# Multiplying every third tap of a depthwise convolution on GpSimd

## The chip, the core and the metric

The kernel runs on one core of one Trainium2 chip. Its engines are TensorE (PE in the profile; PEld is its weight load), VectorE (DVE), ScalarE (ACT), GpSimd (POOL) and SyncE (SP, which issues most transfers). The metric is the device time of one execution in microseconds. A measurement of the kernel is the median of several executions.

## What is computed

The reference is a trunk of two layers over a sequence of 256 positions with 2048 channels, in float32. Each layer normalises the input, modulates it by a vector c, projects it with one matrix into 13 pieces of 512 channels, sends these through four mixers (Fourier, neighbourhood attention, retention, convolution), gates and concatenates the results, and projects them back.

```
for l in range(DEPTH):                                   # 2 layers
    mod = c_act @ w_ada[l] + b_ada[l]                    # (3 x 2048)
    h = _rmsnorm(x, norm_g[l]) * (1.0 + scale) + shift
    z = h @ w_in[l]                                      # 256 x 2048 @ 2048 x 6656
    ...
    o_cv = _conformer_conv(cv_a, cv_b, ...) * silu(cv_g)
    y = concatenate([o_fft, o_na, o_ret, o_cv]) @ w_out[l]
    x = x + gate * y

def _conformer_conv(a, b, conv_w, conv_b, ln_g, ln_b, w_pw):
    u = a * sigmoid(b)
    y = depthwise_conv(u, conv_w, width 31, centred) + conv_b   # 512 channels, each its own 31 weights
    y = layernorm(y) * ln_g + ln_b
    return silu(y) @ w_pw
```

The change lies in the depthwise convolution: y[s, ch] is the sum over 31 taps t of conv_w[t, ch] * u[s + t - 15, ch].

## The kernel before

**Weights.** Nearly all time is matrix products of the normalised input with streamed weights. A weight step loads 256 rows by 512 columns (512 KB) into one of eight buffers named raw. ScalarE casts it to a high part `whi` (line 340), VectorE subtracts that from the loaded values to get a low part `wlo` (line 341), and TensorE makes three products of high and low parts with the high and low parts of the input, `hh` and `hl` (lines 358 to 361 where the result has channels on partitions, 390 to 392 where it has positions there). Four split weight steps can be ahead of TensorE.

**Modulation.** The product of c with w_ada is made on VectorE: each step loads 128 rows of 1024 numbers into the same raw buffers, and one VectorE instruction multiplies them with c, spread over the partitions (`cbc`), and sums (line 515; the row `DVE_READ_ACCUMULATOR2_ANT` belongs to it). These steps are merged between the weight steps.

**The mixers.** Each mixer is a Python generator that is advanced by a pacer once per weight step, so that its instructions lie between those of the weight steps. The convolution starts when its two input pieces are there (`uT`, 128 channels on partitions times 4 blocks of channels, 256 positions with 15 zeros on both sides). Its sum `y` (tile `cy`) has 4 blocks of 256 positions. In the code before, a tap is made in one of two ways:

- Where t is not a multiple of 3, ScalarE multiplies the shifted input by the tap's weight, a number per partition, into a product tile `cvp` of two blocks (128x2x256, line 684; two such buffers take turns), and VectorE adds the product to the sum, two blocks at once (line 688, 128x512).
- Where t is a multiple of 3 and not 0, which is ten taps in a layer, VectorE multiplies and adds in one instruction per block (line 672, 128x256, four of them).

A tap yields to the pacer twice, after half its work and at its end; the pace is 2 yields per weight step in layer 0 and 1.5 in layer 1.

**What sets the order.** The program is written in the order of the generators, and a scheduler then puts each engine's instructions into a fixed order from its own estimate of when they are ready. Each engine works through its list in that order. A change of one instruction's engine can thus move others.

**GpSimd** does little before: some small powers (lines 212, 219, 707, 977), and four pairs of transfers that spread the gates (lines 538 and 540).

Of the kernel before, what the change touches and what calls it, by code (L numbers as in the profile page):

```python
# [11 lines left out]
F32 = mybir.dt.float32  # L12
F32R = mybir.dt.float32r
AF = mybir.ActivationFunctionType
ALU = mybir.AluOpType
AX = mybir.AxisListType

P = 128
S = 256
# [72 lines left out]
def trunk(ctx, tc, x, c, cols, w_ada, w_in, w_fft, na_bias, consts, conv_w_pw, w_out, final_g, out):  # L92
    nc = tc.nc
    V, A, G, T = nc.vector, nc.scalar, nc.gpsimd, nc.tensor

    sb = ctx.enter_context(tc.tile_pool(name="sb", bufs=1))
# [3 lines left out]
    def bank(tag, name):  # L100
        return ps.tile([P, 512], F32, tag=tag, name=name)

    def wide(tag, name):
        return sb.tile([P, 1024], F32, tag=tag, name=name)

    def ta(name, n=512):
        return sb.tile([P, 512], F32, tag="ta", name=name, bufs=3)[:, :n]
# [4 lines left out]
    def small(name, n, bufs=4):  # L112
        return sb.tile([P, n], F32, name=name, bufs=bufs)
# [461 lines left out]
    def h_cva(l, z):  # L575
        def f():
            for b in range(2):
                V.scalar_tensor_tensor(z[b], flags["t"][b], 1.0, z[b], op0=ALU.add, op1=ALU.mult)
            pacer.add("conv", conv(l), PACE["conv"][l])
        later(1, f)  # L580
# [84 lines left out]
    def conv(l):  # L665
        uT = T4[CVA]
        y = wide("cvA", "cy").rearrange("p (k s) -> p k s", k=4)
        w = cwt[:, l].rearrange("p (w k) -> p w k", k=4)
        for t in range(CW):
            if t and t % 3 == 0:  # L670
                for b in range(4):
                    V.scalar_tensor_tensor(y[:, b], uT[:, b, t:t + S], w[:, t, b:b + 1], y[:, b],  # L672
                                           op0=ALU.mult, op1=ALU.add)
                    if b == 1:
                        yield
            else:
                for b in range(0, 4, 2):
                    d = sb.tile([P, 2, S], F32, tag="cvp", name="cvp", bufs=2) if t else y[:, b:b + 2]
                    for i in range(2):
                        if t == 0:  # L680
                            A.activation(d[:, i], uT[:, b + i, 0:S], AF.Identity, scale=w[:, 0, b + i:b + i + 1],
                                         bias=prm[:, 4 * l + b + i:4 * l + b + i + 1])
                        else:
                            A.activation(d[:, i], uT[:, b + i, t:t + S], AF.Copy, scale=w[:, t, b + i:b + i + 1])  # L684
                    if b == 0:
                        yield
                    if t:
                        V.tensor_tensor(y[:, b:b + 2], y[:, b:b + 2], d, op=ALU.add)  # L688
            yield
        yn = wide("cvU", "yn").rearrange("p (m n) -> p m n", m=2)  # L690
        bs, mvs, rss = [], [], []
        yield
        for m in range(2):
            b = bank("mx", "cvt")
            for k in range(4):
                T.transpose(b[:, k * P:(k + 1) * P], y[:, k, m * P:(m + 1) * P], ident)
            bs.append(b)
        yield
        yield
        for m in range(2):  # L700
            st = small("cst", 6)
            mv = small("cmv", 2)
            rs = small("crs", 1)
            V.bn_stats(st, bs[m])
            V.bn_aggr(mv, st)
            V.tensor_scalar(rs, mv[:, 1:2], EPS, None, op0=ALU.add)
            G.tensor_tensor(rs, rs, nhalf[:, :1], op=ALU.pow)
            mvs.append(mv)
            rss.append(rs)
        yield  # L710
        yield
        for m in range(2):
            if m < YNA:
                off = small("cof", 1)
                V.scalar_tensor_tensor(off, mvs[m][:, 0:1], -1.0, rss[m], op0=ALU.mult, op1=ALU.mult)
                A.activation(yn[:, m], bs[m], AF.Identity, scale=rss[m], bias=off)
            else:
                V.tensor_scalar(yn[:, m], bs[m], mvs[m][:, 0:1], rss[m], op0=ALU.subtract, op1=ALU.mult)
        yield
        yield  # L720
        y2 = wide("cvA", "cy2").rearrange("p (k s) -> p k s", k=4)
        for k2 in range(2):
            b = bank("mx", "cvt2").rearrange("p (k s) -> p k s", k=2)
            for k in range(2):
                for m in range(2):
                    T.transpose(b[:, k, m * P:(m + 1) * P], yn[:, m, (2 * k2 + k) * P:(2 * k2 + k + 1) * P], ident)
            t = ta("cth2").rearrange("p (k s) -> p k s", k=2)
            for k in range(2):
                i = 4 * l + 2 * k2 + k
                A.activation(t[:, k], b[:, k], AF.Tanh, scale=lnh[:, i:i + 1], bias=lnh[:, 8 + i:9 + i])  # L730
                A.activation(y2[:, 2 * k2 + k], b[:, k], AF.Identity, scale=prm[:, 8 + i:9 + i],
                             bias=prm[:, 16 + i:17 + i])
            yield
            yield
            V.scalar_tensor_tensor(y2[:, 2 * k2:2 * k2 + 2], t, 1.0, y2[:, 2 * k2:2 * k2 + 2],
                                   op0=ALU.add, op1=ALU.mult)
        while flags.get(CVG) != l or "fft" in pacer.gens:
            yield "wait"
        yield from pointwise(conv_w_pw[l], y2, T4[CVG].rearrange("p (k s) -> p k s", k=4), 0.25)
# [9 lines left out]
    def pointwise(w, y, g, factor):  # L749

        wt = load_small(w)
        for _ in range(4):
            yield
        b = None
        for o in range(4):
            k2, k = divmod(o, 2)
            if k == 0:
                old, b = b, bank("mx", "pwb").rearrange("p (k s) -> p k s", k=2)
            for kt in range(4):
                T.matmul(b[:, k], wt[kt // 2][:, kt % 2, o * P:(o + 1) * P], y[:, kt], start=(kt == 0),  # L760
                         stop=(kt == 3))
            yield
            if k == 1:
                V.scalar_tensor_tensor(g[:, 2 * k2:2 * k2 + 2], b, factor, g[:, 2 * k2:2 * k2 + 2],
                                       op0=ALU.mult, op1=ALU.mult)
# [535 lines left out]
```

## Time and profile before

| | us |
|---|---|
| median of 3 runs | 952.18 |
| lowest and highest run | 949.46, 954.27 |
| profiled execution | 955.11 |
| its span, first to last instruction | 953.3 |
| TensorE busy | 902.8 (95%) |
| VectorE busy | 780.6 (82%) |
| ScalarE busy | 591.0 (62%) |
| GpSimd busy | 22.2 (2%) |
| transfers, mean rate | 272 GB/s |

The profile is one execution. Its page lists busy time of each engine, the span in 40 slices (a digit is the busy share in tenths), the costliest groups of instructions, and the chain of work that ended last. A group's row has the line, the engine, the operation, what it writes and reads, shape and count, then the busy time of the group and the mean of one instruction in ns, then the idle time of the engine just before these instructions and what ended it. Busy time of a group counts overlapping records once. A row of the timeline has start, duration, engine, line and operation; in brackets stands the idle time before it and what released it. A row of waits names who waited for whom, then the total in us, the number of waits and the longest. A table of stretches has, behind the length of the stretch, busy time and number of instructions of each engine.

### The profile page before, as it was taken

The numbers are of one execution on the slowest core, as the hardware profiler recorded it, in microseconds if no ns is written. First come the engines' busy times: TensorE is split into PE (matmuls) and PEld (weight loads), VectorE is DVE, ScalarE is ACT, GpSimd is POOL, SyncE is SP. The second block draws the span as 40 slices with busy tenths as digits, with TensorE's granted clock in tenths as the row PEclk, the third lists the DMA queues.
The fourth block names the chain that finished last, engine by engine and source line by source line (L and its number), as shares of the span: only waits on it lengthen the run. The fifth ranks groups of instructions, "written<-read, shape, count | busy, mean of one in ns | idle before, by whom it ended". The sixth has DMA issues, their size and how long they took to land.

```text
span 953.3 us, 14695 instructions
## 1 busy us (share of the span) xinstructions
PE 902.8 (95%) x5294; PEld 769.1 (81%) x5294; DVE 780.6 (82%) x1266; ACT 591.0 (62%) x1019; POOL 22.2 (2%) x31
## 2 busy tenths in 40 slices
PE   4789999999998999999999999999999999999995
PEld 1779799898976786778878999999778889788874
DVE  5988989889998999888878798558987977578963
ACT  4488855779776766544644464669899645643441
POOL 2000000000000010010000000000000000010000
PEclk6899999999999999999999999999999999999998
DMA  9999997897786777979876999777755576479932
GB/s 338 397 399 376 362 399 276 297 381 246 262 272 237 245 268 264 309 255 337 305 251 194 320 373 381 243 245 231 234 179 163 183 251 188 128 247 328 325 118 88
DMA packets 109068, 259.68 MB, mean 272 GB/s; under 512 B 8386, under 2 KB 10562, under 8 KB 108740
## 3 DMA queue, kind: packets, MB, share of 16 engines
q1 hardware_dynamic: 108292, 256.64, 77.8%
q0 software_dynamic: 704, 2.11, 0.6%
q8 instruction: 41, 0.67, 0.3%
q14 instruction: 31, 0.25, 0.1%
HBM read 256.61 MB, written 2.11 MB: 271 GB/s over the span
## 4 chain that ended last, share of the span: by engine, by line
PE 54%; DMA 18%; DVE 17%; issue 6%; ACT 4%; POOL 1%; DVEq 0%; SPq 0%; POOLq 0%; ACTq 0%
PE acc L361 9%; PE acc L358 9%; PE acc L360 9%; DMA raw<-in_w_in_dram 9%; PE acc L390 7%; PE acc L391 7%; PE acc L392 7%; DVE wlo L341 7%; DMA raw<-in_w_ada_dram 6%; DVE raw L515 4%; DMA raw<-in_w_out_dram 2%; ACT whi L340 1%; PE pwb L760 1%; DMA xs<-in_x_dram 1%; PE nao L828 1%
## 5 line engine op out<-in xcount | busy, mean ns | idle before, releaser
L340 ACT ACTIVATE whi<-raw 128x1024 fp32r<-128x1024 f32 (+1 forms) x272 | 277.6, 1028 | 185.6 <-PE acc L392 89.1
L341 DVE TENSOR_TENSOR wlo<-raw,whi 128x1024 fp32r<-128x1024 f32 (+1 forms) x272 | 319.9, 1182 | 49.4 <-ACT whi L340 47.9
L515 DVE CUSTOM_DVE_ANT_0 raw<-raw,cbc 128x1024 f32<-128x1024 f32 x192 | 232.8, 1221 | 48.4 <-DMA raw<-in_w_ada_dram 48.3
L358 PE MATMUL acc<-hh,whi 128*128 128x256 f32 x896 | 255.8, 286 | 10.1 <-ACT hh L286 7.3
L360 PE MATMUL acc<-hl,whi 128*128 128x256 f32 x896 | 252.7, 283 | 2.4 <-DVE hl L299 2.4
L361 PE MATMUL acc<-hh,wlo 128*128 128x256 f32 x896 | 252.2, 284 | 1.7 <-DVE wlo L341 1.1
L391 PE MATMUL acc<-wlo,hh 128*128 128x512 f32 x600 | 239.5, 399 | 3.0 <-DVE wlo L341 2.8
L390 PE MATMUL acc<-whi,hh 128*128 128x512 f32 x600 | 242.2, 406 | 0.0
L392 PE MATMUL acc<-whi,hl 128*128 128x512 f32 x600 | 238.7, 398 | 0.0
L358 PEld LDWEIGHTS acc<-hh,whi 128*128 128x128 f32 x896 | 169.2, 189 | 15.7 <-ACT hh L286 7.7
L360 PEld LDWEIGHTS acc<-hl,whi 128*128 128x128 f32 x896 | 170.1, 190 | 3.3 <-DVE hl L299 2.7
L361 PEld LDWEIGHTS acc<-hh,wlo 128*128 128x128 f32 x896 | 169.1, 190 | 2.9 <-DVE wlo L341 2.8
L391 PEld LDWEIGHTS acc<-wlo,hh 128*128 128x128 f32 x600 | 114.0, 190 | 31.0 <-DVE wlo L341 5.4
L390 PEld LDWEIGHTS acc<-whi,hh 128*128 128x128 f32 x600 | 113.4, 190 | 29.6 <-issue 4.6
L392 PEld LDWEIGHTS acc<-whi,hl 128*128 128x128 f32 x600 | 113.7, 189 | 27.0
L459 ACT ACTIVATE z<-acc 128x512 f32<-128x512 f32 x99 | 57.4, 598 | 36.1 <-PE acc L361 20.1
L684 ACT ACTIVATE cvp<-uT,constants 128x256 f32<-128x256 f32 x160 | 70.6, 500 | 12.2 <-DVE cy L688 12.1
L688 DVE TENSOR_TENSOR cy<-cy,cvp 128x512 f32<-128x512 f32 x80 | 52.5, 688 | 1.6 <-ACT cvp L684 1.5
L430 ACT ACTIVATE acc<-z 128x512 f32<-128x512 f32 x63 | 36.5, 599 | 0.3
L672 DVE SCALAR_TENSOR_TENSOR cy<-uT,constants,cy 128x256 f32<-128x256 f32 x80 | 34.7, 480 | 0.1
L205 ACT ACTIVATE junk<-xs 128x512 f32<-128x512 f32 x16 | 9.5, 593 | 35.9 <-DVE xs L484 35.9
L483 DVE TENSOR_TENSOR yt<-acc,gate_bc 128x512 f32<-128x512 f32 x16 | 10.4, 684 | 12.5 <-PE acc L392 12.5
(211 smaller groups left out, 703.4 us busy)
## 6 DMA issues: line engine op xcount, KB each, us to landing
raw<-in_w_in_dram SPq DMA_DIRECT2D x198, 512.0 KB, 5.2
raw<-in_w_ada_dram SPq DMA_DIRECT2D x192, 512.0 KB, 6.1
raw<-in_w_out_dram SPq DMA_DIRECT2D x64, 512.0 KB, 6.0
raw<-in_w_in_dram SPq DMA_DIRECT2D x20, 256.0 KB, 6.7
nab<-in_na_bias_dram SPq DMA_DIRECT2D x16, 192.0 KB, 3.6
xs<-in_x_dram SPq DMA_DIRECT2D x2, 1024.0 KB, 5.9
gate_bc<-gate_row POOLq DMA_DIRECT2D x4, 512.0 KB, 5.1
wsm<-in_w_fft_dram SPq DMA_DIRECT2D x4, 512.0 KB, 5.4
```

The source lines that it names most:

```text
L340: self.on_act = A.activation(self.hi[:, :n], self.raw[:, :n], AF.Copy).ins
L341: self.on_dve = V.tensor_tensor(self.lo[:, :n], self.raw[:, :n], self.hi[:, :n].bitcast(F32), op=ALU.subtract).ins
L358: T.matmul(o, wh[:, sl], hh[:, k], start=fresh and blk % 2 == 0 and blk // 2 not in g.seeded, stop=False, skip_group_check=True)
L360: T.matmul(o, wh[:, sl], hl[:, k], start=False, stop=False, skip_group_check=True)
L361: T.matmul(o, wl[:, sl], hh[:, k], start=False, stop=en, skip_group_check=True)
L390: T.matmul(o, hh[:, k, sl], wh, start=st, stop=False, skip_group_check=m in g.seeded)
L391: T.matmul(o, hh[:, k, sl], wl, start=False, stop=False, skip_group_check=m in g.seeded)
L392: T.matmul(o, hl[:, k, sl], wh, start=False, stop=en, skip_group_check=m in g.seeded)
L459: A.activation(o, i, AF.Copy, scale=0.125 if last and self.piece == NAQ else 1.0)
L515: V.tensor_tensor_reduce(w, w, cbc[:, self.half * KH:(self.half + 1) * KH], 0.5, 0.0, ALU.mult, ALU.add, to)
L684: A.activation(d[:, i], uT[:, b + i, t:t + S], AF.Copy, scale=w[:, t, b + i:b + i + 1])
L688: V.tensor_tensor(y[:, b:b + 2], y[:, b:b + 2], d, op=ALU.add)
```

## The change

In the taps that are multiples of 3, the four fused multiply-adds of VectorE are replaced. GpSimd multiplies each of the four blocks by the tap's weight into a product tile, and VectorE adds two blocks at once. The product tiles are called `cvq` and come from the same two buffers as ScalarE's products (tag `cvp`).

```
         for t in range(CW):
             if t and t % 3 == 0:
-                for b in range(4):
-                    V.scalar_tensor_tensor(y[:, b], uT[:, b, t:t + S], w[:, t, b:b + 1], y[:, b],
-                                           op0=ALU.mult, op1=ALU.add)
-                    if b == 1:
+                for b in range(0, 4, 2):
+                    d = sb.tile([P, 2, S], F32, tag="cvp", name="cvq", bufs=2)
+                    for i in range(2):
+                        G.tensor_scalar(d[:, i], uT[:, b + i, t:t + S], w[:, t, b + i:b + i + 1], None, op0=ALU.mult)
+                    if b == 0:
                         yield
+                    V.tensor_tensor(y[:, b:b + 2], y[:, b:b + 2], d, op=ALU.add)
             else:
                 for b in range(0, 4, 2):
                     d = sb.tile([P, 2, S], F32, tag="cvp", name="cvp", bufs=2) if t else y[:, b:b + 2]
```

The lines after it are two further down in the changed kernel: the addition of ScalarE's product is line 688 before and 690 after; GpSimd's product is line 674 and its addition line 677.

The order on VectorE at the start of layer 0's convolution, taps 2 to 6, before:

```order
L688 TENSOR_TENSOR cy<-cy,cvp 128x512 x2
L341 TENSOR_TENSOR wlo<-raw,whi 128x1024
L672 SCALAR_TENSOR_TENSOR cy<-uT,constants,cy 128x256 x4
L341 TENSOR_TENSOR wlo<-raw,whi 128x1024
L688 TENSOR_TENSOR cy<-cy,cvp 128x512 x2
L341 TENSOR_TENSOR wlo<-raw,whi 128x1024
L688 TENSOR_TENSOR cy<-cy,cvp 128x512 x2
L672 SCALAR_TENSOR_TENSOR cy<-uT,constants,cy 128x256
L341 TENSOR_TENSOR wlo<-raw,whi 128x1024
L672 SCALAR_TENSOR_TENSOR cy<-uT,constants,cy 128x256 x3
```

and the same taps after:

```order
L690 TENSOR_TENSOR cy<-cy,cvp 128x512 x2
L341 TENSOR_TENSOR wlo<-raw,whi 128x1024
L677 TENSOR_TENSOR cy<-cy,cvq 128x512 x2
L341 TENSOR_TENSOR wlo<-raw,whi 128x1024
L690 TENSOR_TENSOR cy<-cy,cvp 128x512 x2
L515 ISA raw,msum<-raw,cbc 128x1024
L515 ISA msum 128x1
L341 TENSOR_TENSOR wlo<-raw,whi 128x1024
L690 TENSOR_TENSOR cy<-cy,cvp 128x512 x2
L341 TENSOR_TENSOR wlo<-raw,whi 128x1024
L677 TENSOR_TENSOR cy<-cy,cvq 128x512 x2
```

The additions of GpSimd's products stand where the fused instructions stood, one split (line 341) behind the additions of the tap before; GpSimd can write a product's buffer only after those. One modulation product (line 515) has moved up among them.

The order on GpSimd from the first convolution to the end of layer 0, after:

```order
L674 TENSOR_SCALAR cvq<-uT,constants 128x256 x17
L538 DMA gate_row<-gcol 128x8
L674 TENSOR_SCALAR cvq<-uT,constants 128x256 x3
L540 DMA gate_bc<-gate_row 128x1024
L674 TENSOR_SCALAR cvq<-uT,constants 128x256 x20
L538 DMA gate_row<-gcol 128x8
L540 DMA gate_bc<-gate_row 128x1024
L709 TENSOR_TENSOR crs<-crs,nhalf 128x1 x2
```

Before, the four transfers stood there with nothing between them. Now the first pair stands among the products of the fifth multiplied tap and behind it, and the second pair behind all 40 products of the layer. In layer 1 all 40 products stand ahead of the transfers.

## The prediction

> **What bounds the kernel now.** I read the first two parts of the page, then the two stretches in which the convolution runs, then who waits there, then GpSimd's own rows.
>
> ```profile
> span 953.3 us, 14695 instructions
> PE 902.8 (95%) x5294; PEld 769.1 (81%) x5294; DVE 780.6 (82%) x1266; ACT 591.0 (62%) x1019; POOL 22.2 (2%) x31
> PE   4789999999998999999999999999999999999995
> DVE  5988989889998999888878798558987977578963
> ```
>
> TensorE is busy from the third slice to the last but one. Its ends are modelled, so I also look at how close its matmuls start in the chain of waits, in the first convolution:
>
> ```profile
> 217.06 0.23 PE acc L390
> 217.29 0.23 PE acc L391
> 217.53 0.23 PE acc L392
> ```
>
> They follow each other at 0.23 us with no gap. TensorE is the bound here; another engine costs time only by letting it run dry. The convolution's instructions lie in 205 to 340 us (layer 0) and 640 to 760 us (layer 1). A table of busy time in these two stretches (engines in the order of its first row):
>
> ```profile
> core 0: us, PE busy (x) PEld busy (x) DVE busy (x) ACT busy (x) POOL busy (x), PEclk, DMA share, GB/s
> 205.00:340.00 135.00, 130.51 (x770) 109.68 (x769) 128.37 (x247) 108.29 (x220) 1.85 (x3) 0.99 0.79 263
> 640.00:760.00 120.00, 116.97 (x738) 100.59 (x737) 103.08 (x198) 106.05 (x221) 0.00 (x0) 1.00 0.64 201
> ```
>
> TensorE idles 4.5 us in the first and 3.0 us in the second: 7.5 us is all that a lighter VectorE could win back there. VectorE idles 6.6 us in the first and 16.9 us in the second. In the first it is as full as TensorE, and it decides when the weight buffers come free, since the split into high and low parts (line 341) and the modulation products (line 515) are the last readers of each loaded tile. The chain of waits shows that loop, from a convolution instruction over a split to the next load and the next cast:
>
> ```profile
> 258.65 1.58 DVE cy L672 x4
> 260.24 1.15 DVE wlo L341
> 261.40 6.11 DMA raw<-in_w_in_dram
> 267.59 1.06 ACT whi L340
> ```
>
> So in layer 0 a later VectorE is a later load. In layer 1 its idle time is mostly waiting for inputs:
>
> ```profile
> DVE raw L515 <- DMA raw<-in_w_ada_dram: 6.9, 5, 1.9
> DVE sm L809 <- ACT nasb L804: 3.2, 3, 1.5
> DVE z L833 <- PE nao L828: 2.6, 3, 1.5
> ```
>
> **The change, part by part.** Ten of the 31 taps in each layer (3, 6, ... 30) lose four fused multiply-adds on VectorE and get four multiplications on GpSimd and two additions on VectorE.
>
> ```profile
> L688 DVE TENSOR_TENSOR cy<-cy,cvp 128x512 f32<-128x512 f32 x80 | 52.5, 688 | 1.6 <-ACT cvp L684 1.5
> L672 DVE SCALAR_TENSOR_TENSOR cy<-uT,constants,cy 128x256 f32<-128x256 f32 x80 | 34.7, 480 | 0.1
> ```
>
> Removed: 80 instructions, 34.7 us busy, 0.434 us each where they overlap their neighbours. Added: 40 additions of 128x512, the form of the first row, at 52.5/80 = 0.656 us, so 26.2 us. VectorE's own work falls by 8.5 us, 4.2 us in each layer.
>
> GpSimd gets 80 multiplications of 128x256, a form that this trace does not have. The nearest rows are those where it works over a whole tile, and its one-element multiply, first with VectorE idle and then beside it:
>
> ```profile
> L176 POOL IOTA diff<- 128x384 f32 x1 | 0.4, 448 | 0.0
> masks.py:199 POOL TENSOR_SCALAR_AFFINE_SELECT ident<-ident 128x128 f32<-128x128 f32 x1 | 0.3, 285 | 0.0
> 11.75 0.19 POOL L211 TENSOR_SCALAR ms<-ms 128x1 f32<-128x1 f32 x1
> 15.01 1.06 POOL L211 TENSOR_SCALAR ms<-ms 128x1 f32<-128x1 f32 x1
> 14.80 1.22 DVE L515 CUSTOM_DVE_ANT_0 raw<-raw,cbc 128x1024 f32<-128x1024 f32 x1
> 15.94 1.22 DVE L515 CUSTOM_DVE_ANT_0 raw<-raw,cbc 128x1024 f32<-128x1024 f32 x1
> 17.09 1.22 DVE L515 CUSTOM_DVE_ANT_0 raw<-raw,cbc 128x1024 f32<-128x1024 f32 x1
> ```
>
> Low end: 0.19 us fixed and the affine select's slope, (0.285 - 0.19)/128 per element, is 0.38 us for 256 elements. High end: twice the affine select, 0.57 us. I take 0.45 us, near the middle, since no row favours either end: 40 x 0.45 = 18.0 us of GpSimd in each layer.
>
> The last five rows price what it does to VectorE. The same one-element instruction took 0.19 us with VectorE idle and 1.06 us while VectorE worked on two operands in SBUF: issued at 15.01, it ended at 16.07, just after the VectorE instruction that began at 14.80 gave way to the next at 15.94. GpSimd waited for its turn and got it between two VectorE instructions. VectorE started at 14.80, 15.94 and 17.09, 1.14 and 1.15 us apart, so a one-element GpSimd instruction cost it nothing that shows; what a 256-element one costs it no row shows. The ends are nothing and the whole 0.45 us. I take the whole: what keeps GpSimd out while VectorE works should keep VectorE out while GpSimd works, and where it does not, the addition that needs the product is the next or next but one on VectorE's queue (the rows in the part on the change) and waits for it there. Nearly everything VectorE does in these stretches, line 341, line 515 and the additions, has two operands in SBUF.
>
> The Trainium skill (SBUF — State Buffer, section "Who interferes with whom") goes further than the row: a VectorE instruction with two SBUF inputs and a GpSimd instruction that reads SBUF hold the shared ports in turn, each for its whole instruction. By it VectorE pays the whole 18.0 us in each layer; by the spacing of the VectorE rows alone it would pay nothing. The trace agrees on GpSimd's side (1.06 us against 0.19 us) and does not show VectorE's.
>
> VectorE's sum in each layer is then 18.0 - 4.2 = 13.8 us more (0.38 us: 11.0; 0.57 us: 18.6; no block: 4.2 less). What of it reaches TensorE is what the idle time does not hold. Layer 0: of 6.6 us I count half as usable, 3.3, because much of it is waiting for casts whose loads hang on VectorE itself: 10.5 us reach the end. Layer 1: of 16.9 us I count two thirds, 11.3, because the modulation products and the attention inputs that it waits for come whatever it does: 2.5 us. Together 13.0 us. After 340 us TensorE is full again to the next layer, so nothing is won back.
>
> What costs nothing. The additions use the two product buffers that ScalarE's products use, so ScalarE's next product waits for the addition of GpSimd's product; ScalarE idles 26.7 us of the first stretch and makes a half tap in two products, so this hides as long as the additions are not themselves late. GpSimd's two gate transfers now stand among its products:
>
> ```profile
> 256.68 0.74 POOL L538 DMA_DIRECT2D gate_row<-gcol  x1 [239.10 <-DVE gcol L537]
> 260.43 0.56 POOL L540 DMA_DIRECT2D gate_bc<-gate_row  x1 [3.01 <-ACT cvp L684]
> ```
>
> One product stands behind the first (0.74 us, once). The second, with its 3.0 us of waiting, follows the twentieth product, the end of a tap; the next is needed three taps later, about 12 us (135/31 a tap). In layer 1 the transfers come after the products.
>
> The sum against the profiled execution: 955.1 us (span 953.3 and 1.8 around it) + 13.0 = 968.1 us. That execution was 2.9 us above the median of the runs, 952.18 us; taken off, 965 us.
>
> **The rivals.** All in the median's frame, 952.2.
>
> *The turns are short.* If GpSimd keeps VectorE out only while it moves data, 0.45 - 0.19 = 0.26 us, the sum is 10.4 - 4.2 = 6.2 us in each layer: 2.9 us left in layer 0 and none in layer 1, 955 us. For it: VectorE's start times did not move above. Against it: the additions wait for whole products, not for the shared part. The Trainium skill (GPSIMD Engine Reference, section 4.1 "Engine selection") calls GpSimd's one-input work roughly line-rate; its 1.2 GHz makes that, as an estimate, 0.21 us for 256 elements, and the sum by it is 1.0 us in layer 0 and nothing in layer 1. No row here shows a one-input GpSimd instruction over 256 elements.
>
> *Relief.* If the two do not meet at all, VectorE has 8.5 us less to do. This is the faster side, and it is limited by TensorE's idle time in the two stretches, 7.5 us, whose largest pieces are these, the first two in layer 0:
>
> ```profile
> PE nas L784 <- ACT napt L820: 2.5, 1, 2.5
> PE pwb L760 <- DVE nm L796: 1.1, 1, 1.1
> PE ff L856 <- ACT ffb L872: 1.4, 1, 1.4
> PE ff L856 <- ACT z L459: 1.4, 2, 0.7
> ```
>
> ScalarE's lateness goes back to VectorE through loads like that at 261.40, so I let 6 us fall away: 946 us. For it: VectorE is on the chain in layer 0. Against it: the 1.06 us row, and that most of these waits name ScalarE.
>
> *No slack is usable.* If VectorE's waits move along with it, because the loads it waits for start only when it frees their buffers, as at 260.24 above, both sums arrive whole: 2 x 13.8 = 27.6 us, 980 us. It decides once TensorE has used the split weights made ahead (four tiles). For it: VectorE waits for a modulation tile 6.9 us in layer 1. Against it: in the middle of layer 1's stretch VectorE idles over 3 us in 20 us (third number 16.53 and 16.81), and TensorE is full all the same:
>
> ```profile
> 700.00:720.00 20.00, 19.75 (x103) 14.68 (x102) 16.53 (x47) 19.05 (x47) 0.00 (x0) 1.00 0.52 161
> 720.00:740.00 20.00, 20.00 (x139) 16.46 (x138) 16.81 (x32) 18.94 (x40) 0.00 (x0) 1.00 0.53 159
> ```
>
> **How the numbers follow.** Forecast 0.50 (965 us); short turns 0.25 (955 us); no slack 0.14 (980 us); relief 0.11 (946 us). About 0.5%, 4.8 us, is what a measurement of this kernel can tell from no change: 947.4 to 956.9 us. Slower is the forecast and no slack, 0.64. Same is short turns and the weakest part of relief, 0.02: 0.27. Faster is the rest, 0.09. The range runs from 949, which keeps out most of relief, to 985, the forecast's two sums at the long GpSimd duration with little slack (955.1 + 37.2 - 3.3 - 2.9 = 986). The forecast's own range is 960 to 975, the ends of GpSimd's duration through the same sum: 0.38 us leaves 7.7 us in layer 0 and nothing in layer 1, 0.57 us 15.3 and 7.3 us.
>
> **What would show it.** GpSimd: 80 multiplications, each recorded at 0.4 to 1.3 us, since the wait for the turn is in the record (as in the 1.06 us row). VectorE: 40 additions on GpSimd's products at 0.65 us, and VectorE waiting for GpSimd before them, some 5 to 15 us in all; its splits at line 341 longer than the 1.22 us of now, or starting more than 1.14 us apart, only in the two stretches. The stretch from the first product to the last addition is 10 us longer in layer 0 and 2 to 5 us in layer 1, with TensorE's waits for the low parts of the weights, in layer 0 these two, up from 0.9 us:
>
> ```profile
> PE acc L361 <- DVE wlo L341: 0.7, 1, 0.7
> PE acc L391 <- DVE wlo L341: 0.2, 1, 0.2
> ```
>
> Wrong would be: splits that keep 1.14 us beside GpSimd's products (then relief or short turns), a multiplication far from 0.38 to 0.57 us when VectorE stands still, or a loss that lies outside the two stretches.

## The result

The changed kernel took 982.91 us, median of 3 runs (979.02 to 983.2), against 952.18 us before: a ratio of 1.032 with a 95% interval of 1.029 to 1.036. It is slower by 30.7 us. The prediction was 965 us; the direction was right, the loss more than twice as large. Its profiled execution took 983.2 us. One execution of an experiment below ran at a granted clock of 0.84 instead of 0.98 and is left out of that experiment's median.

The head of its page and three groups of instructions:

```profile
span 981.4 us, 14829 instructions
PE 915.3 (93%) x5294; PEld 777.7 (79%) x5294; DVE 779.6 (79%) x1226; ACT 591.9 (60%) x1019; POOL 129.9 (13%) x111
POOL 2000000024443310010000000004532420010000
L674 POOL TENSOR_SCALAR cvq<-uT,constants 128x256 f32<-128x256 f32 x80 | 106.9, 1350 | 488.7 <-DVE cy L690 471.6 <-DVE gcol L537 8.5 <-ACT whi L340 7.7
L686 ACT ACTIVATE cvp<-uT,constants 128x256 f32<-128x256 f32 x160 | 71.0, 499 | 38.9 <-DVE cy L677 28.8
L677 DVE TENSOR_TENSOR cy<-cy,cvq 128x512 f32<-128x512 f32 x40 | 29.3, 735 | 34.6 <-POOL cvq L674 34.5
```

The last row carries the result. VectorE's 40 additions of GpSimd's products took 29.3 us, but VectorE stood still for 34.5 us in front of them, waiting for GpSimd. GpSimd's 80 multiplications were recorded at 1.35 us each. ScalarE in turn waited 28.8 us for those additions, because the two share product buffers.

The first such tap on VectorE and GpSimd, from the timeline (start, duration, idle time before):

```profile
214.40 1.22 DVE L341 TENSOR_TENSOR wlo<-raw,whi 128x1024 fp32r<-128x1024 f32 x1
217.27 0.96 DVE L677 TENSOR_TENSOR cy<-cy,cvq 128x512 f32<-128x512 f32 x1 [1.66 <-POOL cvq L674]
219.07 0.69 DVE L677 TENSOR_TENSOR cy<-cy,cvq 128x512 f32<-128x512 f32 x1 [0.84 <-POOL cvq L674]
219.68 1.22 DVE L341 TENSOR_TENSOR wlo<-raw,whi 128x1024 fp32r<-128x1024 f32 x1
```

```profile
213.98 2.35 POOL L674 TENSOR_SCALAR cvq<-uT,constants 128x256 f32<-128x256 f32 x1 [195.61 <-DVE cy L690]
216.32 0.92 POOL L674 TENSOR_SCALAR cvq<-uT,constants 128x256 f32<-128x256 f32 x1
217.22 0.92 POOL L674 TENSOR_SCALAR cvq<-uT,constants 128x256 f32<-128x256 f32 x1
218.12 0.92 POOL L674 TENSOR_SCALAR cvq<-uT,constants 128x256 f32<-128x256 f32 x1
```

GpSimd is released at 213.98, when the first of the two shared buffers is free. Its first product takes 2.35 us, because VectorE is working: an addition to 214.40 and then a split to 215.6. The other three take 0.92 us each. VectorE, whose next instruction needs the first two products, is idle from 215.6 to 217.27, and again between the two additions. From the split's start at 214.40 to the next split at 219.68 pass 5.28 us, with one split and the tap. Before, the same piece (a split and four fused instructions) took 1.14 and 1.58 us. The split during which GpSimd's product waits keeps its 1.22 us.

The time was lost in both layers alike. The start of the convolution is marked by line 578, of which the rows for layer 1 read, before and after:

```profile
640.68 0.69 DVE L578 SCALAR_TENSOR_TENSOR uT<-z,uT 128x512 f32<-128x512 f32 x1 [0.59 <-ACT uT L459]
```

```profile
654.41 0.69 DVE L578 SCALAR_TENSOR_TENSOR uT<-z,uT 128x512 f32<-128x512 f32 x1 [0.59 <-ACT uT L459]
```

The same row of layer 0 stands at 206.27 and 204.10 us. So from the first convolution to the second 434.4 us became 450.3 us (15.9 more), and from there to the end of the span 312.6 us became 327.0 us (14.4 more).

TensorE ran dry behind the queues of VectorE and ScalarE. In layer 1 its two longest waits were these:

```profile
708.25 1.22 PE L858 MATMUL ff<-constants,z 128*128 128x256 f32 x2 [3.60 <-ACT z L459]
791.62 0.33 PE L637 MATMUL rt<-ident,rot 128*128 128x128 f32 x1 [4.66 <-DVE rot L627]
```

The first one waits for a copy on ScalarE, which had itself waited 0.74 us, at 703.31, for the addition of a GpSimd product. The second one waits for VectorE's rotation, which stands on VectorE's queue behind additions of GpSimd products. The nearest of these, at 786.88, had its product in time; the two before it, at 776.49 and 778.83, had waited 0.83 and 1.24 us. Summed over the whole trace, TensorE's waits for VectorE grew from 15.9 to 25.3 us and those for ScalarE from 24.0 to 29.5 us. Its waits for the splits (line 341), which are among the first, grew only from 3.9 to 5.2 us.

The gaps are only about half of the loss. These are the stretches from the first convolution to the second and from there to the end, before and after (the first busy time is TensorE's, the third VectorE's, and the number behind the last count is the granted clock):

```profile
206.27:640.68 434.41, 423.13 (x2498) 361.23 (x2497) 366.99 (x593) 267.44 (x461) 9.70 (x9) 1.00 0.82 280
640.68:953.30 312.62, 298.23 (x1649) 248.25 (x1647) 237.20 (x384) 190.14 (x348) 7.44 (x9) 0.99 0.63 206
```

```profile
204.10:654.41 450.31, 431.13 (x2498) 367.45 (x2497) 366.46 (x574) 267.92 (x461) 65.54 (x49) 0.98 0.80 271
654.41:981.40 326.99, 303.71 (x1649) 251.34 (x1647) 236.91 (x364) 190.77 (x348) 59.35 (x49) 0.97 0.61 196
```

TensorE's idle time grew by 7.9 and 8.9 us. The same number of matmuls also kept it busy for 8.0 and 5.5 us longer, at a lower granted clock. Over the whole execution busy time times granted clock did not change: 902.8 x 0.979 = 883.8 before, 915.3 x 0.966 = 884.2 after. Slow matmuls stand right behind the longest gaps, as here in layer 0:

```profile
299.83 2.95 PE L786 MATMUL nas<-z 64*128 64x256 f32 x8 [3.91 <-DVE z L766]
303.30 0.63 PE L391 MATMUL acc<-wlo,hh 128*128 128x512 f32 x1
303.73 0.63 PE L392 MATMUL acc<-whi,hl 128*128 128x512 f32 x1
308.82 0.39 PE L390 MATMUL acc<-whi,hh 128*128 128x512 f32 x1
309.05 0.39 PE L391 MATMUL acc<-wlo,hh 128*128 128x512 f32 x1
```

Behind the gap of 3.91 us these matmuls start 0.43 us apart, and five microseconds later 0.23 us apart again. That the gap brings the slow matmuls is read from this order in time; no run here has the one without the other.

### The profile page after: what moved, and what is told of

It is laid out like the page before. It is cut to its first block, busy times and chain, and to the rows that moved or that the text cites. A ratio compares the mean times of both kernels' runs of the same rounds, so it can differ in the third digit from the quotient of the medians.

```text
span 981.4 us, 14829 instructions
## 1 busy us (share of the span) xinstructions
PE 915.3 (93%) x5294; PEld 777.7 (79%) x5294; DVE 779.6 (79%) x1226; ACT 591.9 (60%) x1019; POOL 129.9 (13%) x111
## 4 chain that ended last, share of the span: by engine, by line
PE 28%; DVE 15%; DMA 12%; issue 8%; ACT 5%; POOL 5%; DVEq 0%; POOLq 0%; ACTq 0%
DMA raw<-in_w_ada_dram 7%; DVE wlo L341 6%; PE acc L358 4%; PE acc L360 4%; PE acc L361 4%; PE acc L390 4%; PE acc L391 4%; PE acc L392 4%; POOL cvq L674 4%; DMA raw<-in_w_in_dram 3%; DVE raw L515 3%; DMA raw<-in_w_out_dram 2%; ACT whi L340 2%; DVE cy L690 1%; DVE yt L483 1%
## 5 line engine op out<-in xcount | busy, mean ns | idle before, releaser
L390 PE MATMUL acc<-whi,hh 128*128 128x512 f32 x600 | 244.8, 410 | 0.0
L674 POOL TENSOR_SCALAR cvq<-uT,constants 128x256 f32<-128x256 f32 x80 | 106.9, 1350 | 488.7 <-DVE cy L690 471.6
L392 PEld LDWEIGHTS acc<-whi,hl 128*128 128x128 f32 x600 | 115.0, 192 | 27.6
L686 ACT ACTIVATE cvp<-uT,constants 128x256 f32<-128x256 f32 x160 | 71.0, 499 | 38.9 <-DVE cy L677 28.8
L677 DVE TENSOR_TENSOR cy<-cy,cvq 128x512 f32<-128x512 f32 x40 | 29.3, 735 | 34.6 <-POOL cvq L674 34.5
```

The lines of the kernel that those rows point to most:

```text
L390: T.matmul(o, hh[:, k, sl], wh, start=st, stop=False, skip_group_check=m in g.seeded)
L392: T.matmul(o, hl[:, k, sl], wh, start=False, stop=en, skip_group_check=m in g.seeded)
L674: G.tensor_scalar(d[:, i], uT[:, b + i, t:t + S], w[:, t, b + i:b + i + 1], None, op0=ALU.mult)
```

## The experiments

Two theories were set against each other at first. A: GpSimd's product is slow, the shared buffers let it start late, and VectorE waits for it. B: the two engines keep each other out for the whole of a product. Each time stands beside runs of the kernel before on the same chip (medians 951.4 to 953.0 us).

### GpSimd's product in its own buffer

```
-                    d = sb.tile([P, 2, S], F32, tag="cvp", name="cvq", bufs=2)
+                    if b == 0:
+                        qt = wide("rk", "cvq").rearrange("p (k s) -> p k s", k=4)
+                    d = qt[:, b:b + 2]
```

> GpSimd's product gets its own buffer (one tile of four blocks that is free during the convolution) instead of one of the two that ScalarE's products use. Then GpSimd can multiply tap t as soon as the additions of tap t-3 are done, two taps ahead, and ScalarE does not wait for it. Theory A (VectorE waits for a slow product because the shared pair of buffers lets GpSimd start too late; the two engines hinder each other only for some 0.2 us a product): VectorE's waits for products fall from 34.5 us to under 6 us, and the time from 983 us to 952 to 964 us. Theory B (each product keeps VectorE out for its whole 0.92 us): VectorE's waits turn into longer VectorE instructions, busy time 30 us or more up, and the time stays at 972 to 986 us.

956.01 us, a ratio of 1.0033 (1.0013 to 1.0053). The additions now wait for nearly nothing, while the products are recorded longer than ever:

```profile
L676 POOL TENSOR_SCALAR cvq<-uT,constants 128x256 f32<-128x256 f32 x80 | 139.6, 1759 | 413.8 <-DVE uT L578 323.4 <-DVE cy L679 90.4
L679 DVE TENSOR_TENSOR cy<-cy,cvq 128x512 f32<-128x512 f32 x40 | 26.8, 692 | 1.2 <-POOL cvq L676 0.7
```

VectorE's waits fell from 34.5 us to 0.7 us, and 27 of the 31 us came back. The number of products, their engine and the additions are the same. So most of the loss hung on the waiting and not on the meeting of the engines: theory A, whose ranges held. The order of VectorE's queue moved in places as well. ScalarE, too, was freed by this edit (the additions of GpSimd's products no longer hold its buffers), so this run alone does not say which of the two waits cost.

### The meeting of the engines alone

```
                 for b in range(4):
+                    if b == 0:
+                        q = wide("rk", "cvq").rearrange("p (k s) -> p k s", k=4)
+                    G.tensor_scalar(q[:, b], uT[:, b, t:t + S], w[:, t, b:b + 1], None, op0=ALU.mult)
                     V.scalar_tensor_tensor(y[:, b], uT[:, b, t:t + S], w[:, t, b:b + 1], y[:, b],
```

> The kernel before, with the fused multiply-adds kept on VectorE, plus the same 80 GpSimd multiplications into a tile that nothing reads. Nobody waits for a product, so only the meeting of the two engines is left, and VectorE is not relieved. Theory A: VectorE's busy time grows by 80 x 0.2 to 0.28 us, 16 to 22 us, and the time by half of that or less: 955 to 965 us. Theory B: by 80 x 0.92 us, 74 us, and the time to over 985 us. If the engines do not meet at all: 950 to 954 us.

960.96 us, 1.0094 (1.0068 to 1.012). The page of this run:

```profile
PE 906.1 (94%) x5294; PEld 770.0 (80%) x5294; DVE 792.6 (82%) x1266; ACT 591.3 (61%) x1019; POOL 152.9 (16%) x111
```

VectorE's busy time is 792.6 us against 780.6 us: 12.0 us more, 0.15 us for each of the 80 products, less than A had expected and a sixth of a product's 0.92 us. The time rose by 8.9 us, three quarters of that, where A had expected half or less. The meeting is thus not free, even where nobody waits for a product. How a meeting looks, from the first of them:

```profile
206.45 1.42 DVE L341 TENSOR_TENSOR wlo<-raw,whi 128x1024 fp32r<-128x1024 f32 x1
207.80 1.21 DVE L515 CUSTOM_DVE_ANT_0 raw<-raw,cbc 128x1024 f32<-128x1024 f32 x1
```

```profile
204.90 2.36 POOL L674 TENSOR_SCALAR cvq<-uT,constants 128x256 f32<-128x256 f32 x1 [186.79 <-DVE uT L578]
207.25 3.73 POOL L674 TENSOR_SCALAR cvq<-uT,constants 128x256 f32<-128x256 f32 x2
```

The split during which the first product ends takes 1.42 us instead of 1.22; the modulation product after it is not longer. The product itself stretches from 0.92 to 2.36 us. The two are not symmetrical: here VectorE loses 0.2 us, and GpSimd loses one VectorE instruction or more.

### VectorE's relief alone

```
-                    d = sb.tile([P, 2, S], F32, tag="cvp", name="cvq", bufs=2)
-                    for i in range(2):
-                        G.tensor_scalar(d[:, i], uT[:, b + i, t:t + S], w[:, t, b + i:b + i + 1], None, op0=ALU.mult)
...
-                    V.tensor_tensor(y[:, b:b + 2], y[:, b:b + 2], d, op=ALU.add)
+                    V.tensor_tensor(y[:, b:b + 2], y[:, b:b + 2], uT[:, b:b + 2, t:t + S], op=ALU.add)
```

> The ten taps add the shifted input itself and no product is made (their multiplications are left out), so that only VectorE's relief is left: 40 additions instead of 80 fused instructions, 8.5 us less VectorE work. If VectorE's load decides in the two stretches: 944 to 948 us. If TensorE is the bound whatever VectorE does there: 949 to 953 us.

950.24 us, 0.9959 (0.9938 to 0.9979). VectorE was busy 773.3 us, 7.3 us less. By the medians 1.9 us of it reached the end, by the interval 2 to 6 us. The median lies in the range for TensorE as the bound. So with this order of the queues at most 6 us were to be won from the start, and probably less.

### What a GpSimd multiplication takes

```
+    for n in (64, 128, 256, 512):
+        po = sb.tile([P, 1024], F32, tag="nak", ...)
+        G.tensor_scalar(po[:, :n], pin[:, :n], psc[:, 0:1], None, op0=ALU.mult)
+    for n in (256, 512):
+        ...
+        G.tensor_scalar(po[:, :n], pin[:, :n], 0.5, None, op0=ALU.mult)
```

> The kernel before, plus six GpSimd multiplications of 128xN on scratch data at the very start, with VectorE nearly idle: N = 64, 128, 256, 512 with a scalar per partition, N = 256 and 512 with a constant. In the changed kernel the shortest 128x256 took 0.91 us. If that is mostly a cost per element: about 0.35, 0.55, 0.92 and 1.65 us. If mostly fixed: all within 0.6 to 1.2 us. If the per-partition scalar makes it slow: the two with a constant take 0.4 to 0.6 us.

GpSimd's timeline at the start of this kernel (start, duration):

```profile
1.40 0.28 POOL masks.py:199 TENSOR_SCALAR_AFFINE_SELECT ident<-ident 128x128 f32<-128x128 f32 x1
2.73 0.45 POOL L184 TENSOR_SCALAR ppa<-pin,psc 128x64 f32<-128x64 f32 x1 [1.05 <-DVE ssq L1177]
3.29 0.60 POOL L184 TENSOR_SCALAR ppb<-pin,psc 128x128 f32<-128x128 f32 x1
3.98 0.92 POOL L184 TENSOR_SCALAR ppd<-pin,psc 128x256 f32<-128x256 f32 x1
5.00 1.56 POOL L184 TENSOR_SCALAR pph<-pin,psc 128x512 f32<-128x512 f32 x1
6.65 0.85 POOL L187 TENSOR_SCALAR pid<-pin 128x256 f32<-128x256 f32 x1
7.59 1.49 POOL L187 TENSOR_SCALAR pih<-pin 128x512 f32<-128x512 f32 x1
```

It is mostly a cost per element: from 64 to 512 elements (1.56 - 0.45)/448 = 2.5 ns an element, and about 0.29 us fixed. The 0.92 us of the changed kernel's shortest products is thus the plain cost of 256 elements with VectorE out of the way. A constant instead of a scalar per partition saves 0.07 us. The affine select of 128 elements, from which the prediction took its slope, takes 0.28 us where the multiply takes 0.60 us.

### Half a product

```
-                        G.tensor_scalar(d[:, i], uT[:, b + i, t:t + S], ...)
+                        G.tensor_scalar(d[:, i, :P], uT[:, b + i, t:t + P], ...)
...
-                    V.tensor_tensor(y[:, b:b + 2], y[:, b:b + 2], d, op=ALU.add)
+                    y4 = y[:, b:b + 2].rearrange("p k (h s) -> p k h s", h=2)
+                    V.tensor_tensor(y4, y4, d[:, :, None, :P].to_broadcast([P, 2, 2, P]), op=ALU.add)
```

> The changed kernel with GpSimd's product made for the first 128 of the 256 positions only; the addition keeps its size and adds that half twice (the products for positions 128 to 255 are left out). Order and buffers stay. By the probe a product then takes 0.60 us instead of 0.92 us. Theory A (VectorE stands and waits for the product's own duration): 4 x 0.32 = 1.28 us less in each of 20 taps, 25.6 us at most: 957 to 967 us, VectorE's waits for products 8 to 18 us instead of 34.5. Theory C (the price is the handing over of the two shared buffers among ScalarE, GpSimd and VectorE and the new order, whatever a product takes): 973 to 984 us.

966.83 us, 1.0152 (1.0104 to 1.02). With buffers as in the changed kernel and only the product shorter:

```profile
L674 POOL TENSOR_SCALAR cvq<-uT,constants 128x128 f32<-128x128 f32 x80 | 78.8, 998 | 499.6 <-DVE cy L691 481.6 <-ACT whi L340 8.7 <-DVE gcol L537 8.5
L678 DVE TENSOR_TENSOR cy<-cy,cvq 128x512 f32<-128x512 f32 x40 | 29.0, 728 | 18.8 <-POOL cvq L674 18.7
```

VectorE's waits fell to 18.7 us (a little above what A had named) and the loss from 30.7 to 15.4 us, at the upper end of A's range. The price follows the product's duration, so it is not the handing over as such (theory C). ScalarE's waits for the additions of these products fell with it, from 28.8 to 17.4 us.

### One buffer of its own

```
-                    d = sb.tile([P, 2, S], F32, tag="cvp", name="cvq", bufs=2)
+                    d = wide("rk", "cvq")[:, :512].rearrange("p (k s) -> p k s", k=2)
```

> GpSimd's product gets one buffer of half a tap (two blocks) of its own, ScalarE keeps its pair to itself. GpSimd can make a tap's first half early, but the second half only after the first has been added. Theory A: VectorE still waits for two products of 0.92 us in each tap, so 20 x 1.7 = 34 us of waits at most, 20 or more, and 968 to 982 us. Theory C (ScalarE's waiting for its pair, 28.8 us in the changed kernel, is what costs): ScalarE's waits fall to those of before and the time to 953 to 962 us.

973.45 us, 1.0244 (1.0199 to 1.0289), as A had it: VectorE waited 28.0 us for products. It was to show as well what ScalarE's waiting costs, and does not: ScalarE still waited 26.7 us for its pair, now for VectorE's additions of its own products (line 690), which came late behind the waits. The two waits could not be taken apart.

### GpSimd's products in layer 1 only

```
-            if t and t % 3 == 0:
+            if t and t % 3 == 0 and l == 0:
+                for b in range(4):
+                    V.scalar_tensor_tensor(...)      # as before the change
+                    if b == 1:
+                        yield
+            elif t and t % 3 == 0:
```

> GpSimd's products in layer 1 only; layer 0 keeps the fused instructions. As the prediction had it, layer 1's 16.9 us of VectorE idle time take up most of it: 954 to 959 us. If none of that idle time is usable, because VectorE stands at the head of its queue and what TensorE needs stands behind it: 13 to 17 us, 964 to 970 us.

968.08 us, 1.0176 (1.0132 to 1.0219): 16.6 us for layer 1 alone, where the prediction had left 2.5 us. VectorE waited 17.0 us for products there. It was idle 188.0 us in the whole execution against 172.7 us before, so its other idle time took up only 1.7 us of these waits.

The waits and the losses side by side (loss against the kernel before on the same chip):

| kernel | VectorE waits for products, us | loss, us |
|---|---|---|
| the change | 34.5 | 30.7 |
| one buffer of its own | 28.0 | 22.0 |
| half a product | 18.7 | 15.4 |
| layer 1 only | 17.0 | 16.6 |
| two half-tap buffers of its own | 0.7 | 3.9 |

In the first four rows there are 0.8 to 1 us of loss for each microsecond of waiting. The last row has 3.9 us of loss with hardly a wait, so part of each loss is the meeting. The three losses from 15 to 22 us are known to about 4 us. The order of VectorE's queue changed too, most with one buffer of its own and in layer 1 only; half a product left it nearly as in the changed kernel, and so shows best that the waiting follows the product's duration.

### ScalarE makes all products

```
-            if t and t % 3 == 0:
+            if t and t % 3 == 0 and False:        # in the kernel before: every tap goes to ScalarE
```

> ScalarE makes all products, GpSimd none: the same relief of VectorE as in the changed kernel (8.5 us) with an engine that does not meet VectorE, and 80 more ScalarE products (0.44 us each, 35 us; it idles 27 us and 14 us in the two stretches of before). If ScalarE has room: 948 to 952 us, as without products. If ScalarE fills up, its casts come late: 955 to 970 us.

941.25 us, 0.9901 (0.987 to 0.9933): faster than both kernels, and by 7 us more than had been expected. VectorE's work is that of the run without products (773.3 us busy in both), and ScalarE does 28 us more, yet the time is lower than without any products (9 us by the medians, 6 us by the two ratios). The gain that follows the change lies in layer 0: from the first convolution to the second the profiled execution took 423.1 us (203.15 to 626.30) against 434.4 us, and from there on 312.2 us against 312.6 us. TensorE's idle time in the first of these fell from 11.3 to 3.8 us. In layer 0's stretch (205 to 345 us) ScalarE waited less for weight loads; the row before:

```profile
ACT whi L340 <- DMA raw<-in_w_in_dram: 17.5, 14, 2.7
```

and with all products on ScalarE:

```profile
ACT whi L340 <- DMA raw<-in_w_in_dram: 4.0, 3, 2.0
```

Without products it was 20.5 us. The order on VectorE differs as well: when ScalarE has ten more taps to make, the scheduler puts the modulation products further ahead of the additions in the first half of layer 0's convolution. At the tenth tap 80 of them stand ahead instead of 76; from the twentieth tap on the two orders are level or one behind. VectorE is the last reader of a loaded tile, so this frees buffers for loads earlier.

### The modulation products ahead, without ScalarE's help, and with it

```
             to = msum[:, self.l, self.which, self.half, self.k:self.k + 1]
-            V.tensor_tensor_reduce(w, w, cbc[...], 0.5, 0.0, ALU.mult, ALU.add, to)
+            with tc.high_priority(offset=100):
+                V.tensor_tensor_reduce(w, w, cbc[...], 0.5, 0.0, ALU.mult, ALU.add, to)
```

> The kernel before, with the modulation products (line 515) given a higher priority in the scheduler, so that they stand further ahead on VectorE's queue; in the version with ScalarE's products they stand up to four places further ahead at the ninth tap of layer 0 too. Engines and work as before. Theory E (ScalarE's version gains because VectorE frees the loaded tiles earlier, so that loads come earlier): 943 to 949 us, ScalarE's waits for weight loads in layer 0's stretch down from 17.5 us to under 8 us. Theory F (it gains by the work it moves, not by the order): 950 to 954 us.

949.79 us, 0.9972 (0.9953 to 0.999). This lies between the ranges of the two theories. ScalarE's waits for loads in the stretch fell to 10.1 us, short of what E had named, and 0.1 to 0.5% was won: the direction of theory E, less than a third of the gain of ScalarE's version. At the tenth tap 79 modulation products stand ahead here, so nearly the same lead did not bring the same gain.

> ScalarE makes all products, and the modulation products have the higher priority as well. Theory E: little beyond ScalarE's version, 938 to 943 us, since most of them stand ahead there already. If VectorE's splits come too late behind them: 945 us or more.

948.26 us, 0.9949 (0.993 to 0.9967), outside what E had named and in the range for splits that come too late. TensorE's waits for splits did grow, from 1.5 us with ScalarE's products alone to 4.2 us, which is part of the 7 us. With this edit on top, the version with ScalarE's products lost most of its gain, though ScalarE waited for no weight load in the stretch any more. So the order of VectorE's queue moves this kernel by several microseconds in both directions, but "earlier modulation products, earlier loads" does not account for the 941 us. What makes that order better is open.

## Why the prediction was right or wrong

- **TensorE as the bound, VectorE on the chain in layer 0.** Right in the main: VectorE's relief alone was worth 2 to 6 us, against 6 us in the rival case. One reading was wrong. After 340 us TensorE is not full to the next layer; it idles 6.8 us from there to the second convolution.
- **VectorE's own work.** Right: predicted 8.5 us less; without products it was 7.3 us less.
- **GpSimd's duration.** Wrong: 0.45 us, with ends of 0.38 and 0.57 us, against 0.92 us with VectorE out of the way. The step that failed here is the slope taken from the affine select (0.7 ns an element, where the multiply has 2.5), and the upper end was twice that instruction again. Two rows of other operations bounded nothing.
- **What a product costs VectorE.** The size was near by luck, the form was not right. Forecast was the whole product, 36.0 us for 80, as time in which VectorE is kept out. Measured were 34.5 us of waiting and 6.3 us of longer instructions (busy 779.6 us against 773.3 us without products). A product took twice as long as thought, 80 x 0.92 = 73.6 us, and about half of that was hidden behind other work. VectorE's sum was 33.5 us more instead of 27.6 us. The sentence that the addition waits for the product where the engines do not exclude each other was the one that held, and it deserved its own term: the first such tap needs four products, 3.7 us, and had one split, 1.14 us, to hide them.
- **The rule of the shared ports.** The Trainium skill (SBUF — State Buffer, section "Who interferes with whom") has each engine hold the ports for its whole instruction. The runs agree on GpSimd's side: beside VectorE's work products stretch to 2.96 us in the changed kernel, and to 3.50 us with a buffer of their own. They differ on VectorE's: 0.15 us for each product of 0.92 us where nothing waits for the product, so here the measurement decides.
- **From VectorE's sum to TensorE.** This is the step that failed, in two terms. First, 3.3 us of VectorE's idle time in layer 0 and 11.3 us in layer 1 were counted as usable, so that 10.5 and 2.5 us would reach the end. In the changed kernel VectorE's sum was 17.7 us in layer 0 and 16.0 us in layer 1, and 15.9 and 14.4 us of these reached the end: the idle time held 1.8 and 1.6 us. The run with products in layer 1 alone lost 16.6 us. Second, another engine was to cost time only by letting TensorE run dry, and TensorE's own time was held fixed. Its gaps grew by 7.9 us in layer 0, less than the 10.5 us forecast, and by 8.9 us in layer 1; but its matmuls also took 8.0 and 5.5 us longer at the lower granted clock, a term that the prediction does not have.
- **Why the idle time held so little.** VectorE works through its queue in order, and while it waits at an addition, everything behind it waits too. TensorE's waits were mostly for results of the mixers, such as the rotation, and only 1.3 us more for the low parts of the weights, by which the prediction let the lateness travel. That VectorE's old idle time lies at other places on the queue, where the inputs were late, is the likely reason that it did not help; no run moved it.
- **Work said to cost nothing.** ScalarE's next product was to hide; it waited 28.8 us for the new additions. TensorE's waits for ScalarE grew by 5.5 us and those for VectorE by 9.4 us, so part of the loss passed through ScalarE. What its waiting cost beyond VectorE's own could not be separated. The gate transfers cost what was said: the first took 0.76 us between two products.
- **The rivals.** "No slack is usable" gave 980 us and came nearest. Its statement, that the sums arrive whole, nearly held. Its reason, loads that move along, did not: VectorE waited 40.0 us for modulation tiles in the changed kernel against 48.3 us before. That its time came so near is luck too, since it has neither the product's true duration nor the slower matmuls. The range, 949 to 985 us, held the time.
- **What was to show it.** The additions themselves and the longer stretches were there: from the first such tap to the last addition 13.8 us more in layer 0, where 10 was forecast, and 23.2 us in layer 1, where 2 to 5 was forecast (there the last addition also stands further back in the queue, behind the rotation). GpSimd's records went beyond 1.3 us and VectorE's waits beyond 15 us. Most splits stayed at 1.22 us, a few took 1.4 us (1.42 at 755.53, 1.41 at 787.48). So two of the signs of being wrong appeared: splits that keep their length, and a multiplication far from 0.38 to 0.57 us.

## What to carry to other kernels

Before work goes to another engine, compare the duration of one piece there with the work that stands between its release and its use on the waiting engine's queue; where the buffers force the release to be late, much of the duration is paid (34.5 of 73.6 us here), and a buffer of its own for the whole tap can return nearly all of it (27 of 31 us here). Do not subtract a share of an in-order engine's idle time from a new wait: here 3.4 us of it helped where 14.6 us had been counted. Look at the granted clock as well as at the gaps of the engine that bounds the kernel: here 13.5 us of the loss were longer matmuls. Where the engine to be relieved is not the bound, measure first what its relief alone is worth: here 2 to 6 us.

## What was not expected

- A GpSimd multiplication of 128xN float32 takes 0.29 us and 2.5 ns an element (0.45, 0.60, 0.92 and 1.56 us for 64, 128, 256 and 512), the same within 0.07 us with a constant.
- Beside a busy VectorE the same instruction of 256 elements takes up to 2.96 us in the changed kernel (1.35 us on average) and up to 3.50 us with a buffer of its own. A VectorE instruction with two operands in SBUF is longer by 0.2 to 0.3 us when it is hit (1.42 us instead of 1.22, 0.96 instead of 0.69), and VectorE's work by 0.15 us on average for each product. VectorE can start its next instruction before the waiting GpSimd does: the product released at 213.98 let a whole split go ahead of it.
- TensorE's matmuls of 128x512 start 0.43 us apart behind a gap of 3.91 us and 0.23 us apart five microseconds later. In the changed kernel its busy time grew by 12.5 us with the number of matmuls unchanged, as much as its granted clock fell (0.979 to 0.966).
- Making all products on ScalarE, 28 us more work there, gave 941.25 us, 6 to 9 us below the run with no products for these taps. The gain lies in layer 0 and goes with an order of VectorE's queue in which ScalarE waits 4.0 us for weight loads instead of 17.5 us; moving one kind of instruction forward by hand did not reproduce it.
